# The last eight row tiles of w_down and a second first pair without Strassen, w_down's other blocks two at a time

## The chip, the cores and the metric

The kernel runs on one core of a Trainium2 chip, in one launch. The metric is the device time of one execution in microseconds (us); lower is better. The kernel before took 2080.86 us (median of three runs, 2079.91 to 2081.47).

## What is computed

One layer of a decoder for N = 1056 tokens (1024 of one prompt and 32 of eight samples), D = 1024 features: a SwiGLU half, a token mixer, a second SwiGLU half and a final RMSNorm. In the reference, cut to what the change touches:

```
mod = (silu(c) @ w_ada + b_ada).reshape(B, 9, 1024)
hn = modulate(rmsnorm(x, g_ffn1), mod[0], mod[1])
x  = x + 0.5 * mod[2] * ((silu(hn @ w1_gate) * (hn @ w1_up)) @ w1_down)    # w_gate, w_up 1024x3072, w_down 3072x1024
hn = modulate(rmsnorm(x, g_mix), mod[3], mod[4])
x  = x + mod[5] * (mixer(hn) @ w_mix_out)
hn = modulate(rmsnorm(x, g_ffn2), mod[6], mod[7])
x  = x + 0.5 * mod[8] * ((silu(hn @ w2_gate) * (hn @ w2_up)) @ w2_down)
y  = rmsnorm(x, final_gain)
```

modulate is h * (1 + scale) + shift; every sequence has a conditioning vector c of its own.

## The kernel before

Everything lies feature-major: features on 128 partitions, tokens along the free axis. A float32 operand is split into a high part (an ACT copy to fp32r) and a low part (a DVE subtraction), and a product is three matmuls: high x low, low x high, high x high. The class Stream loads weights through SP's queue into raw buffers and splits them into hl tiles a few units ahead of their use (L175 on ACT, L176 on DVE).

**FFN1 and FFN2.** The feature tiles of 128 go in twelve pairs. In FFN1 the first pair is multiplied directly (first_pair); all later pairs, and all twelve of FFN2, go by Strassen-Winograd (strassen, matmul L365): the operands are cut in 2 x 2 quarters, the token halves being 528 wide, and seven products take the place of eight. A product is 24 matmuls of 264 columns where four tiles of 128 are summed (nk = 4). The hn tiles (hn11, hn21, hn22 and the sums hnT1 to hnT4; hm in FFN2) are the token forms; in FFN2 token_forms (L560 to L579) makes the sums on ACT and DVE from x after the norm. gate_up takes all seven products of the gate (ga) and then all seven of up, and combine (L374 to L384) takes them out of three double PSUM tiles a, c, b: ACT copies the first three (L378), DVE adds later ones to the copies (L383). The results, or their seven token forms, are stored to HBM (store, L650 to L674, on POOL's queue).

**w_down** reads these forms back in groups of feature tiles (GROUPS, L78): pairs 0 to 3, 4 to 7 and 8 to 9, by Strassen with nk = 4, 4 and 2. Within a group the block o = 0 to 3 gives two of the eight output tiles. load_form (L713 to L721) reads a form of the next group, 1056 KB, as soon as the last block's product has freed its buffer, and splits it (ACT L720, DVE L721). down takes the seven products out by combine into temporaries, and adds these to x (L584 and, for the first token half, L758; L588 and L590 for the samples). x itself was dropped during gate and up and is loaded again (L792) into the place of gate_up's temporaries. The last pairs, 10 and 11 (LAST_PAIR), are four row tiles of w_down multiplied directly, by back_by_span over spans of tokens (bk, matmul L327 of 352 columns), so that the next norm can begin on the first span while PE works on the others. last_m (L762 to L771) loads and splits what they multiply (ml).

**Beside it** runs the modulation: ada steps (L408) of eight matmuls each, one every third product, from weights of their own (raw<-wada).

**From the mixer to FFN2** back_by_span goes by quarters of 264 tokens (QUARTERS); x is normed in place into hm and kept (L530 to L535), then token_forms makes the sums, and FFN2's pair 0 begins (ga0).

The order on each engine is the order of the program as a tile scheduler leaves it; every engine runs its own list in order. The diff touches:

Of the kernel before, what the change touches and what calls it, by code (L numbers as in the profile page):

```python
# [14 lines left out]
P = 128  # L15
# [6 lines left out]
N = T + S  # L22
# [55 lines left out]
GROUPS = ((0, 4), (4, 4), (8, 2))  # L78
LAST_PAIR = 10
# [3 lines left out]
class Stream:  # L83


    def __init__(self, nc, rawp, hlp, sums, raw_bufs, plan, srcs):
# [3 lines left out]
        for kind, idx in plan:  # L90
            if kind in ("ga1", "ga2", "dn1", "dn2"):
                self.add_strassen(kind, idx, srcs[kind](idx))
                continue
            b = dict(key=(kind, idx), src=srcs[kind](idx), raw=None, ids=[])
            if kind in ("gu1", "mi"):
# [17 lines left out]
        self.dma = self.split = self.done = self.pos = 0  # L113

    def add_strassen(self, kind, idx, srcs):

        at = len(self.blocks)
        nk = srcs[0].shape[-2]
        blocks = list(range(at, at + len(srcs)))
        for i, src in enumerate(srcs):  # L120
            self.blocks.append(dict(key=(kind, idx) if i == 0 else None, src=src, raw=None, ids=[], left=1,
                                    shape=list(src.shape)))
        self.blocks[at]["ids"] = list(range(len(self.units), len(self.units) + 7))
        self.blocks[at]["span"] = len(srcs)
        sums = {}

        def quarter(raws, m, k):
            return raws[k][:, m - 1] if len(raws) == 2 else raws[0][:, k, m - 1]

        def make(form):  # L130
            def f(raws):
                if form in ("11", "12", "22"):
                    return quarter(raws if len(raws) > 1 else raws * len(blocks), int(form[0]), int(form[1]) - 1)
                w11, w12, w21, w22 = (quarter(raws, m, k) for m in (1, 2) for k in (0, 1))
                t = self.sums(f"{form}_{kind}_{at}", nk * P).rearrange("p (k m) -> p k m", k=nk)
# [11 lines left out]
            return f  # L147

        for form in W_FORMS:
            ends = {"S3": blocks[:1] if len(blocks) == 2 else [], "22": blocks[-1:]}.get(form, [])  # L150
            self.units.append(dict(needs=blocks[:1] if form == "11" else blocks, make=make(form), ends=ends, n=nk))

    def dma_ahead(self):
        while self.dma < min(self.done + self.raw_bufs, len(self.blocks)):
            b = self.blocks[self.dma]
            raw = self.rawp.tile(b["shape"], F32, tag="raw", name=f"raw{self.dma}")
            self.nc.sync.dma_start(raw, b["src"])
            b["raw"] = raw
            self.dma += 1
# [7 lines left out]
    def split_to(self, u):  # L167
        while self.split <= min(u, len(self.units) - 1):
# [5 lines left out]
            hl = self.hlp.tile([P, 2, un["n"], P], F32R, tag="hl", name=f"hl{self.split}")  # L174
# [20 lines left out]
def decoder_step(ctx, tc, xin, par, ada0, ada1, ada2, wada, wf, wga1, wga2, wdn1, wdt, wdl, wmi, wgt, wmo,  # L195
# [17 lines left out]
    hlp = open_pool("hlp", bufs=8)  # L213
# [13 lines left out]
    def strassen_banks(on):  # L227

        nonlocal psp
        if not on:  # L230
            close_pool("ps2")
        close_pool("psp")
        if on:
            psp = open_pool("psp", bufs=2, space=bass.MemoryType.PSUM)
            ps2[0] = open_pool("ps2", bufs=3, space=bass.MemoryType.PSUM)
        else:
            psp = open_pool("psp", bufs=8, space=bass.MemoryType.PSUM)
# [33 lines left out]
    def plan_ffn(n):  # L271
        if n == 1:
            plan.extend(("gu1", (i, w)) for i in range(2) for w in range(2))
        plan.extend((f"ga{n}", (p, w)) for p in range(int(n == 1), NP) for w in range(2))
        plan.extend((f"dn{n}", (g, o)) for g in range(len(GROUPS)) for o in range(4))
        plan.extend((f"d{n}", h) for h in range(4))
# [10 lines left out]
    def down_src(n):  # L287
        def f(i):
            g, o = i
            return [wdn1[n, g, o, 0], wdn1[n, g, o, 1]] if GROUPS[g][1] == 4 else [wdt[n, o]]  # L290
        return f

    ws = Stream(nc, rawp, hlp, lambda name, width: tmp(name, width), 2, plan, dict(
        gu1=lambda i: wf[i[0], i[1]], ga1=lambda i: [wga1[i[0] - 1, i[1], h] for h in range(2)],
        ga2=lambda i: [wga2[i[0], i[1], h] for h in range(2)], dn1=down_src(0), dn2=down_src(1),
        d1=lambda h: wdl[0, h], d2=lambda h: wdl[1, h],
# [50 lines left out]
    def halves(b):  # L347
        return b[:, :, 0:Q]

    def two(t):  # L350
        return t.rearrange("p (q c) -> p q c", q=2)

    def strassen(name, ids, forms, nk, after, done=lambda i: None):

        banks = {}
        for i in range(7):
            hl = ws.unit(ids[i], AHEAD_S)
            new = BANK_OF[i] not in banks
            if new:
                banks[BANK_OF[i]] = ps2[0].tile([P, 2, 512], F32, tag="ps2", name=f"{name}_{BANK_OF[i]}")  # L360
            b = banks[BANK_OF[i]]
            for q in range(2):
                for k in range(nk):
                    for j, (wh, h) in enumerate(((0, 0), (0, 1), (1, 0))):
                        pe.matmul(b[:, q, 0:Q], hl[:, wh, k], forms[X_FORMS[i]][:, k, h, q * Q:q * Q + Q],  # L365
                                  start=new and k == 0 and j == 0, stop=k == nk - 1 and j == 2, skip_group_check=True)
            after(i, banks)
            done(i)
            advance()
# [980 lines left out]
```

## Time and profile before

| | |
|---|---|
| median of three runs | 2080.86 us |
| the profiled execution: its own time | 2083.96 us |
| its span | 2082.0 us |
| PE, DVE, ACT, POOL busy | 95%, 65%, 39%, 6% of the span |
| time by kind of DMA | f<-mf 1056 KB: 7.5 us to landing; raw<-wga 512 KB: 3.4 us |

A row of the timeline is one run of like instructions on an engine: start, duration, line, tiles, count, and in brackets the idle time just before it and what ended it. The rows of PE tell where its work stood still; the windows tell which engine was busy there.

### The profile page before, as it was taken

The page shows a single profiled execution, that of the slowest core. Times are in us where ns is not written, and L with a number is a line of the kernel's source. Part 1 is how long each engine was busy: PE and PEld are TensorE (multiplying, and loading weights), DVE is VectorE, ACT ScalarE, POOL GpSimd, SP SyncE. Part 2 cuts the span into 40 slices and gives each one's busy share as a digit, 9 for nine tenths or more (in the row PEclk, how much of TensorE's full clock was granted, in tenths as well). Part 3 has the DMA queues.
Part 4 walks back from the last instruction along what each step waited for, and adds up shares of the span by engine and source line. Part 5 has one row for each costly group of instructions (what it writes and reads, how often), then busy time and mean ns, then how long its engine had stood idle before and what let it go on. Part 6 is the DMA issues. An engine that isn't in the chain of part 4 may idle for free.

```text
span 2082.0 us, 36792 instructions
## 1 busy us (share of the span) xinstructions
PE 1975.9 (95%) x15256; PEld 1922.7 (92%) x15256; DVE 1361.1 (65%) x2633; ACT 806.6 (39%) x1435; POOL 132.8 (6%) x233
## 2 busy tenths in 40 slices
PE   5999999999989898999999986999999999999897
PEld 4989999999979898999999984999999999999897
DVE  6864554655466758776767788556555655777686
ACT  5433332333343425444434334333333333443453
POOL 0010000010020000000000000001000100110100
PEclk9999999999989999999999996999999999999998
DMA  7144333444381413110111111422222322751312
GB/s 281 37 174 144 138 129 128 145 149 147 122 309 61 179 59 147 63 56 26 51 51 42 53 63 72 148 88 106 106 88 88 124 88 93 271 184 62 148 52 84
DMA packets 70998, 237.18 MB, mean 114 GB/s; under 512 B 7952, under 2 KB 14096, under 8 KB 70832
## 3 DMA queue, kind: packets, MB, share of 16 engines
q1 hardware_dynamic: 44128, 137.40, 19.3%
q0 software_dynamic: 26704, 97.45, 12.6%
q8 instruction: 119, 1.95, 0.4%
q14 instruction: 47, 0.39, 0.1%
HBM read 183.88 MB, written 50.93 MB: 113 GB/s over the span
## 4 chain that ended last, share of the span: by engine, by line
PE 80%; DVE 9%; issue 6%; DMA 4%; ACT 1%; POOL 0%; DVEq 0%; SPq 0%; ACTq 0%; POOLq 0%
PE ga_a L365 13%; PE up_a L365 12%; PE bk L327 9%; PE dn_a L365 7%; PE ga_c L365 6%; PE up_c L365 6%; PE dn_c L365 3%; PE ga_b L365 3%; PE up_b L365 3%; PE v L327 2%; PE b L327 2%; PE c L327 2%; PE x L327 2%; DMA f<-mf 2%; PE ada L408 2%
## 5 line engine op out<-in xcount | busy, mean ns | idle before, releaser
L175 ACT ACTIVATE hl<-raw 128x512 fp32r<-128x512 f32 (+1 forms) x292 | 174.0, 610 | 308.6 <-PE up_a L365 68.6
L365 PE MATMUL dn_a<-f,hl 128*128 128x264 f32 x1920 | 254.5, 289 | 22.9 <-ACT f L720 10.6
L176 DVE TENSOR_TENSOR hl<-raw,hl 128x512 fp32r<-128x512 f32 (+1 forms) x292 | 191.3, 667 | 127.1 <-ACT hl L175 125.8
L365 PEld LDWEIGHTS dn_a<-f,hl 128*128 128x128 f32 x1920 | 243.6, 191 | 27.8 <-ACT f L720 11.0
L176 DVE TENSOR_TENSOR hl<-S_ga,hl 128x512 fp32r<-128x512 f32 x184 | 126.1, 690 | 114.8 <-ACT hl L175 113.7
L175 ACT ACTIVATE hl<-S_ga 128x512 fp32r<-128x512 f32 x184 | 115.5, 629 | 158.2 <-issue 57.2
L365 PE MATMUL dn_c<-f,hl 128*128 128x264 f32 x960 | 133.7, 296 | 7.8 <-DVE d_3st L383 7.5
L365 PEld LDWEIGHTS dn_c<-f,hl 128*128 128x128 f32 x960 | 127.3, 198 | 10.8 <-issue 5.4
L175 ACT ACTIVATE hl<-S_dn 128x512 fp32r<-128x512 f32 (+1 forms) x96 | 53.0, 559 | 175.5 <-DVE x L590 73.3
L365 PE MATMUL ga_a<-hmT,hl 128*128 128x264 f32 x864 | 113.0, 287 | 2.8 <-ACT g0st L378 2.8
L365 PEld LDWEIGHTS ga_a<-hmT,hl 128*128 128x128 f32 x864 | 109.1, 190 | 3.9 <-ACT g0st L378 3.1
L365 PE MATMUL up_a<-hmT,hl 128*128 128x264 f32 x864 | 111.6, 285 | 0.7 <-DVE u11st L383 0.7
L365 PEld LDWEIGHTS up_a<-hmT,hl 128*128 128x128 f32 x864 | 107.7, 188 | 1.9 <-DVE u11st L383 0.9
L365 PEld LDWEIGHTS up_a<-hnT,hl 128*128 128x128 f32 x792 | 100.0, 191 | 6.8 <-issue 4.5
L365 PE MATMUL up_a<-hnT,hl 128*128 128x264 f32 x792 | 104.6, 289 | 1.8 <-DVE u11st L383 1.8
L365 PE MATMUL ga_a<-hnT,hl 128*128 128x264 f32 x792 | 103.0, 286 | 0.0
L365 PEld LDWEIGHTS ga_a<-hnT,hl 128*128 128x128 f32 x792 | 98.5, 188 | 4.5 <-issue 4.5
L721 DVE TENSOR_TENSOR f<-f 128x1056 fp32r<-128x1056 f32 x70 | 85.6, 1255 | 22.0 <-ACT f L720 21.8
L327 PE MATMUL bk<-ml,hl 128*128 128x352 f32 (+2 forms) x672 | 97.5, 305 | 0.0
L327 PEld LDWEIGHTS bk<-ml,hl 128*128 128x128 f32 x672 | 95.1, 192 | 0.0
L720 ACT ACTIVATE f<-f 128x1056 fp32r<-128x1056 f32 x70 | 72.8, 1078 | 42.5 <-DMA f<-mf 42.4
L584 DVE SCALAR_TENSOR_TENSOR x<-bk,modT,x 128x352 f32<-128x352 f32 (+6 forms) x112 | 56.5, 520 | 40.0 <-PE bk L327 39.3
(492 smaller groups left out, 3841.6 us busy)
## 6 DMA issues: line engine op xcount, KB each, us to landing
raw<-wga SPq DMA_DIRECT2D x92, 512.0 KB, 3.4
f<-mf POOLq DMA_DIRECT2D x28, 1056.0 KB, 7.5
raw<-wada SPq DMA_DIRECT2D x56, 512.0 KB, 3.4
raw<-wdn SPq DMA_DIRECT2D x32, 512.0 KB, 3.4
mf<-mt POOLq DMA_DIRECT2D x60, 264.0 KB, 3.5
raw<-wmi SPq DMA_DIRECT2D x20, 512.0 KB, 3.3
f<-mf POOLq DMA_DIRECT2D x14, 528.0 KB, 8.3
raw<-ada SPq DMA_DIRECT2D x16, 384.0 KB, 7.9
```

Source lines behind the costliest of these rows:

```text
L175: self.nc.scalar.activation(hl[:, 0], src, AF.Copy)
L176: self.nc.vector.tensor_sub(hl[:, 1], src, hl[:, 0].bitcast(F32))
L327: pe.matmul(b[:, :sp[1]], hl[:, wh, k], rhs(k, h, sp), start=first and k == ks[0] and i == 0, stop=last and k == ks[-1] and i == 2)
L365: pe.matmul(b[:, q, 0:Q], hl[:, wh, k], forms[X_FORMS[i]][:, k, h, q * Q:q * Q + Q], start=new and k == 0 and j == 0, stop=k == nk - 1 and ...
L408: pe.matmul(ada_bank[u][32 * q:32 * q + 32, :ADA_W[u]], cst[:, k], raw[:, q], start=k == 0, stop=k == KD - 1, skip_group_check=True)
L584: dve.scalar_tensor_tensor(x[:, o, lo:lo + n], b[:, :n], modT[:, buf, GATE, o, 0:1], x[:, o, lo:lo + n], op0=ALU.mult, op1=ALU.add)
L720: act.activation(form[:, k:k + 2, 0], raw[:, k:k + 2], AF.Copy)
L721: dve.tensor_sub(form[:, k:k + 2, 1], raw[:, k:k + 2], form[:, k:k + 2, 0].bitcast(F32))
```

## The change

Four things, in both FFNs where nothing else is said:

1. w_down's last eight row tiles instead of four are multiplied directly: the group of pairs 8 and 9 (nk = 2) is gone, and its four row tiles go by back in spans of 352 columns ahead of back_by_span on the other four.
2. FFN2's first pair is multiplied directly, too (second_pair), quarter by quarter as the norm of each quarter is flushed; the token forms T1, T2 and T4 are made as side work of it, T3 behind it (third_form).
3. strassen takes two jobs side by side: product i of the one, then product i of the other, out of four double PSUM tiles. So go w_down's blocks o and o + 1, and the last pair's gate and up. A double PSUM tile is now read as 528 columns in one piece, and a product of w_down is added to x straight from it, wherever it belongs, so that the copies, temporaries and adds of combine fall away there.
4. The kept copy of the normed x (L535) goes from DVE to ACT; five raw buffers in place of two during an FFN's Strassen part; six hl buffers (eight outside); three ada steps a call in place of two, so that none is left after pair 8.

```diff
-GROUPS = ((0, 4), (4, 4), (8, 2))
-LAST_PAIR = 10
+GROUPS = ((0, 4), (4, 4))
+LAST_PAIR = 8
...
-    hlp = open_pool("hlp", bufs=8)
+    hlp = open_pool("hlp", bufs=6)
...
-            ps2[0] = open_pool("ps2", bufs=3, space=bass.MemoryType.PSUM)
+            ps2[0] = open_pool("ps2", bufs=doubles, space=bass.MemoryType.PSUM)
...
+            ws.rotate("raw", [rawp] * 2 + [open_pool("raw2", bufs=3)] * 3)
+            ws.raw_bufs = 5
...
-    def strassen(name, ids, forms, nk, after, done=lambda i: None):
+    def strassen(jobs, forms, nk, done=lambda i: None):
...
-        banks = {}
+        banks = [{} for _ in jobs]
         for i in range(7):
-            hl = ws.unit(ids[i], AHEAD_S)
...
+            for (name, ids, after), bs in zip(jobs, banks):
+                hl = ws.unit(ids[i], AHEAD_S + len(jobs) - 1)
...
+                after(i, bs)
+                advance()
+                if len(adas[1]) > adas[2] and i % 2 == 1:
+                    more_ada()
             done(i)
-            advance()
-            if len(adas[1]) > adas[2] and i % 3 == 1:
-                more_ada()
...
         if keep:
-            dve.tensor_scalar_add(h, h, shift)
+            act.activation(h, h, AF.Identity, bias=shift)
...
-            for o in range(4):
-                temps = {}
...
-                def add(i, banks):
-                    r = combine(temps, fresh, i, banks)
-                    if r:
-                        f, h, t = r
-                        add_half(buf, 2 * o + f, h, two(t) if i < 6 else t, t if i < 6 else None)
+            for o in (0, 2):
+                ids = ws.take(f"dn{n}", ((g, o), (g, o + 1)))
...
+                def add(o):
+                    def after(i, banks):
+                        f, hs = ((0, (0,)), (1, (1,)), (0, (1,)), (0, (1,)), (1, (1,)), (0, (0,)), (1, (0,)))[i]
+                        for h in hs:
+                            add_back(buf, 2 * o + f, (h * HALF, HALF), whole(banks[BANK_OF[i]]))
+                    return after
...
+                strassen([(f"dn{g}_{o + j}", ids[j], add(o + j)) for j in range(2)], forms, nk, done)
             forms = nxt
...
-        down(n, buf, nxt, ms, form_pools)
-        close_pool("f2")
-        strassen_banks(False)
-        last(f"d{n}", buf, ms[0])
+        down(n, buf, nxt)
...
+        ms = [last_m(m0, n, 0), last_m(mps[0], n, 1)]
+        strassen_banks(0)
+        back(f"d{n}", 0, buf, ms[0])
+        close_pool("m0")
+        last(f"d{n}", buf, ms[1])
...
+    def second_pair():
+        ms = [[(wide if i == 0 else lambda name: tmp(name, HALF))(f"n{i}_{h}") for h in range(2)] for i in range(2)]
+        ids = [[ws.take("gu2", (i, w)) for w in range(2)] for i in range(2)]
+        for c, sp in enumerate(QUARTERS):
+            flush(("n", sp))
+            if c % 2:
+                side.append((("tf", c), token_forms(forms, c // 2, Q)))
+            for i in range(2):
...
+                for w in range(2):
+                    j = 2 * (2 * i + w)
+                    gb, = from_hn(ids[i][w], f"n{i}{w}", [sp], (min(AHEAD, 6 - j), 0, 0, 6)[c])
+                    if w == 0:
+                        act.activation(m, gb[:, :Q], AF.Silu)
+                    else:
+                        dve.tensor_mul(m, m, gb[:, :Q])
+        flush()
+        return [*ms[0], *ms[1]]
```

Three places show how the instructions move. First TensorE in w_down's group 0 (before: the end of block 0 and the start of block 1; `dn0_1_c` is bank c of block 1, `f1_0_2` the third form of group 0 in FFN1):

```order
L365 MATMUL dn0_0_a_6434<-f1_0_4_6296,hl166_6463 128x264 x24
L365 MATMUL dn0_0_b_6595<-f1_0_5_6340,hl167_6495 128x264 x24
L365 MATMUL dn0_0_a_6434<-f1_0_6_6376,hl168_6524 128x264 x24
L365 MATMUL dn0_1_a_6657<-f1_0_0_6143,hl169_6558 128x264 x24
L365 MATMUL dn0_1_c_6691<-f1_0_1_6183,hl170_6592 128x264 x24
L365 MATMUL dn0_1_a_6657<-f1_0_2_6224,hl171_6624 128x264 x24
L365 MATMUL dn0_1_c_6691<-f1_0_3_6261,hl172_6654 128x264 x24
```

and of the changed kernel, blocks 2 and 3 of the same group:

```order
L396 MATMUL dn0_2_a_6879<-f1_0_0_5997,hl176_6756 128x264 x24
L396 MATMUL dn0_3_a_6910<-f1_0_0_5997,hl177_6785 128x264 x24
L396 MATMUL dn0_2_c_6947<-f1_0_1_6067,hl178_6816 128x264 x24
L396 MATMUL dn0_3_c_6981<-f1_0_1_6067,hl179_6846 128x264 x24
L396 MATMUL dn0_2_a_6879<-f1_0_2_6139,hl180_6876 128x264 x24
L396 MATMUL dn0_3_a_6910<-f1_0_2_6139,hl181_6907 128x264 x24
L396 MATMUL dn0_2_c_6947<-f1_0_3_6203,hl182_6944 128x264 x24
L396 MATMUL dn0_3_c_6981<-f1_0_3_6203,hl183_6978 128x264 x24
```

Each form is now used by two products in a row, and two products of other banks lie between two on the same bank.

Next VectorE where group 0's last blocks run and group 1's forms are split (`f1_1_0 x2` is one form's two subtractions; `d0_3st2` a temporary of combine). Before:

```order
L721 TENSOR_TENSOR f1_1_0_7130<-f1_1_0_7130 128x2x528 x2
L383 TENSOR_TENSOR d0_3st2_7203<-dn0_3_c_7143,d0_3st2_7203 128x528
L721 TENSOR_TENSOR f1_1_1_7170<-f1_1_1_7170 128x2x528 x2
L584 SCALAR_TENSOR_TENSOR x1_6417<-d0_3st2_7203,modT_81,x1_6417 128x496
L588 TENSOR_TENSOR ab6_7242<-d0_3st2_7203,modT_81 128x32
L383 TENSOR_TENSOR d0_3st1_7168<-dn0_3_a_7103,d0_3st1_7168 128x528
L721 TENSOR_TENSOR f1_1_2_7205<-f1_1_2_7205 128x2x528 x2
L590 TENSOR_TENSOR x1_6417<-x1_6417,ab6_7242 128x32
L584 SCALAR_TENSOR_TENSOR x1_6417<-d0_3st1_7168,modT_81,x1_6417 128x496
```

and the changed kernel:

```order
L758 TENSOR_TENSOR f1_1_1_7010<-f1_1_1_7010 128x2x528 x2
L193 TENSOR_TENSOR hl185_7053<-S3_dn1_52_1_7051,hl185_7053 128x512
L626 TENSOR_TENSOR ab6_7083<-dn0_3_a_6910,modT_81 128x32
L193 TENSOR_TENSOR hl186_7092<-raw54_6598,hl186_7092 128x512
L628 TENSOR_TENSOR x1_6419<-x1_6419,ab6_7083 128x32
L622 SCALAR_TENSOR_TENSOR x1_6419<-dn0_2_c_6947,modT_81,x1_6419 128x496
L626 TENSOR_TENSOR ab4_7120<-dn0_2_c_6947,modT_81 128x32
L193 TENSOR_TENSOR hl187_7123<-raw55_6693,hl187_7123 128x512
L628 TENSOR_TENSOR x1_6419<-x1_6419,ab4_7120 128x32
L622 SCALAR_TENSOR_TENSOR x1_6419<-dn0_3_c_6981,modT_81,x1_6419 128x496
L758 TENSOR_TENSOR f1_1_2_7086<-f1_1_2_7086 128x2x528 x2
```

Before, one or two places lie from one form's split to the next, with combine's add and the add to x as an instruction each; now nine lie between two forms, the splits of weights among them, and the source of each add to x is PSUM.

Last TensorE between the mixer's last product and FFN2 (`nrm792` and `rb792` belong to the norm of the last quarter; `hl312` and the like are split weights). Before:

```order
L472 MATMUL nrm792_13060<-ones_79,sq792_7_13050 128x1
L493 MATMUL rb792_13093<-dg792_13077,ones_79 128x128 x2
L493 MATMUL rb792_13093<-dg792_13077,ones_79 128x8
L365 MATMUL ga0_a_13286<-hm11_12326,hl312_12968 128x264 x24
L365 MATMUL ga0_c_13320<-hmT1_13139,hl313_13002 128x264 x24
L365 MATMUL ga0_a_13286<-hmT2_13140,hl314_13031 128x264 x20
L408 MATMUL ada9_13347<-raw0_13270,cst_83 32x256 x4
L365 MATMUL ga0_a_13286<-hmT2_13140,hl314_13031 128x264 x4
```

and the changed kernel, where `n01_0` is the first tile's up product on the quarter that begins at token 0:

```order
L504 MATMUL nrm792_12947<-ones_79,sq792_7_12885 128x1
L357 MATMUL n01_0_12973<-hm21_12153,hl295_12906 128x264 x9
L357 MATMUL n10_0_13015<-hm11_12151,hl296_12911 128x264 x12
L357 MATMUL n10_0_13015<-hm21_12153,hl297_12930 128x264 x12
L525 MATMUL rb792_13028<-dg792_12964,ones_79 128x128 x2
L525 MATMUL rb792_13028<-dg792_12964,ones_79 128x8
L357 MATMUL n11_0_13054<-hm11_12151,hl298_12974 128x264 x12
L357 MATMUL n11_0_13054<-hm21_12153,hl299_12993 128x264 x12
L357 MATMUL n00_528_13091<-hm12_12157,hl292_12805 128x264 x12
```

Products on the earlier quarters now lie ahead of, between and behind the steps of the last quarter's norm; before, the first product that needs no sum of quarters stands behind all of them, and the second needs hmT1.

## Rows read from the trace of the kernel before

**Rows 1.** The page, its part 1: busy time, share of the span, instructions.

```profile
PE 1975.9 (95%) x15256; PEld 1922.7 (92%) x15256; DVE 1361.1 (65%) x2633; ACT 806.6 (39%) x1435; POOL 132.8 (6%) x233
```

**Rows 2.** Windows; columns: window, length, PE, PEld, DVE, ACT, POOL busy (instructions), clock, DMA.

```profile
680.00:714.00 34.00, 26.41 (x189) 25.38 (x189) 29.32 (x38) 19.73 (x25) 3.00 (x4) 0.90 0.61 225
...
780.00:815.00 35.00, 27.62 (x198) 25.91 (x197) 31.44 (x57) 19.67 (x32) 4.99 (x8) 0.90 0.52 196
...
1240.00:1260.00 20.00, 11.08 (x65) 10.54 (x63) 18.22 (x59) 7.14 (x16) 0.84 (x1) 0.74 0.16 56
...
1260.00:1280.00 20.00, 8.02 (x18) 4.74 (x18) 19.97 (x60) 10.59 (x26) 0.00 (x0) 0.61 0.00 0
...
1955.00:1985.00 30.00, 22.67 (x150) 21.14 (x149) 26.14 (x42) 18.16 (x28) 4.87 (x7) 0.83 0.54 210
```

**Rows 3.** Timeline of PE, first Strassen product of FFN1.

```profile
108.82 5.50 PE L365 MATMUL ga_c<-hnT,hl 128*128 128x264 f32 x24 [7.56 <-DVE m L861]
```

**Rows 4.** Timeline of PE, FFN1's last up, and the first blocks of w_down.

```profile
570.20 3.09 PE L365 MATMUL up_a<-hn,hl 128*128 128x264 f32 x24
...
573.13 3.09 PE L365 MATMUL up_c<-hnT,hl 128*128 128x264 f32 x24
...
576.14 0.64 PE L408 MATMUL ada<-raw,cst 128*32 128x256 f32 x8
...
606.44 1.08 PE L408 MATMUL ada<-raw,cst 128*32 128x256 f32 x8 [3.78 <-DMA raw<-wada]
```

**Rows 5.** Timeline of PE, change from group 0 to 1, and the direct tiles.

```profile
699.46 5.43 PE L365 MATMUL dn_c<-f,hl 128*128 128x264 f32 x24 [3.77 <-DVE d_3st L383]
...
835.67 4.54 PE L327 MATMUL bk<-ml,hl 128*128 128x352 f32 x27
...
835.83 19.41 PE L327 MATMUL bk<-ml,hl 128*128 128x352 f32 x119
```

**Rows 6.** Timeline of PE, FFN2's last up, group 1 to 2, and the direct tiles.

```profile
1761.43 3.09 PE L365 MATMUL up_a<-hm,hl 128*128 128x264 f32 x24
...
1963.85 0.59 PE L365 MATMUL dn_a<-f,hl 128*128 128x264 f32 x1 [5.51 <-ACT f L720]
...
2011.33 3.84 PE L327 MATMUL bk<-ml,hl 128*128 128x272 f32 x29
```

**Rows 7.** Timeline of PE, from the mixer's last product to FFN2's pair 1.

```profile
1241.45 0.53 PE L327 MATMUL bk<-mix_s,hl 128*128 128x264 f32 x3
...
1255.45 4.10 PE L365 MATMUL ga_a<-hm,hl 128*128 128x264 f32 x24
...
1288.62 4.05 PE L365 MATMUL ga_a<-hmT,hl 128*128 128x264 f32 x20 [2.81 <-ACT g0st L378]
...
1328.20 3.09 PE L365 MATMUL ga_a<-hm,hl 128*128 128x264 f32 x24
```

**Rows 8.** Groups of DVE's instructions by form: busy, mean ns, idle.

```profile
L721 DVE TENSOR_TENSOR f<-f 128x1056 fp32r<-128x1056 f32 x70 | 85.6, 1255 | 22.0 <-ACT f L720 21.8
...
L758 DVE SCALAR_TENSOR_TENSOR x<-dn_a,modT,x 128x528 f32<-128x528 f32 x24 | 18.3, 764 | 0.0
...
L584 DVE SCALAR_TENSOR_TENSOR x<-d_0st,modT,x 128x496 f32<-128x496 f32 x12 | 8.8, 732 | 2.1 <-issue 1.9
...
L579 DVE TENSOR_TENSOR hmT<-t2f,hmT 128x264 fp32r<-128x264 f32 x16 | 7.1, 442 | 0.0
...
L535 DVE TENSOR_SCALAR x<-x,modT 128x264 f32<-128x264 f32 x24 | 8.4, 352 | 0.0
```

**Rows 9.** Timeline of POOL and DVE, FFN2's load of x.

```profile
1787.77 0.71 DVE L703 TENSOR_TENSOR g11s<-g11s,up_a 128x528 f32<-128x528 f32 x1
...
1793.84 4.34 POOL L792 DMA_DIRECT2D x<-xmid  x8 [3.51 <-DMA ml<-g11st]
...
1799.45 0.73 DVE L584 SCALAR_TENSOR_TENSOR x<-d_0st,modT,x 128x496 f32<-128x496 f32 x1 [1.86 <-issue]
```

**Rows 10.** View of the tile ml, in FFN1's w_down.

```profile
DMA to landing us min/median/max: 6.5/6.5/6.5
```

More of the change, by code (lines that the diff above doesn't have):

```diff
@@ L113, in __init__, with rotate, maker, make @@
         self.dma = self.split = self.done = self.pos = 0
+        self.slots = dict(raw=[[rawp], 0], hl=[[hlp], 0])
+    def rotate(self, tag, more=None):
+        s = self.slots[tag]
+        if more is not None:
+            s[:] = [more, 0]
+            return
+        s[1] += 1
+        return s[0][(s[1] - 1) % len(s[0])]
     def add_strassen(self, kind, idx, srcs):
         at = len(self.blocks)
[L118 to L131, printed above, removed]
+        nj = len(srcs)
+        nk = srcs[0][0].shape[-2]
+        for k in range(2):
+            for src in srcs:
+                self.blocks.append(dict(key=None, src=src[k], raw=None, left=1, pair=True, shape=list(src[k].shape)))
+        first = self.blocks[at]
+        first.update(key=(kind, idx), span=2 * nj, ids=[[len(self.units) + nj * i + j for i in range(7)] for j in range(nj)])
+        def maker(j):
+            sums = {}
+            def make(form, raws):
                 if form in ("11", "12", "22"):
-                    return quarter(raws if len(raws) > 1 else raws * len(blocks), int(form[0]), int(form[1]) - 1)
-                w11, w12, w21, w22 = (quarter(raws, m, k) for m in (1, 2) for k in (0, 1))
-                t = self.sums(f"{form}_{kind}_{at}", nk * P).rearrange("p (k m) -> p k m", k=nk)
+                    return raws[-1 if form[1] == "2" else 0][:, int(form[0]) - 1]
+                w11, w12, w21, w22 = (raws[k][:, m] for m in range(2) for k in range(2))
+                t = self.sums(f"{form}_{kind}_{at}_{j}", nk * P).rearrange("p (k m) -> p k m", k=nk)
                 sub, add = self.nc.vector.tensor_sub, self.nc.vector.tensor_add
@@ L155, in dma_ahead @@
             b = self.blocks[self.dma]
-            raw = self.rawp.tile(b["shape"], F32, tag="raw", name=f"raw{self.dma}")
+            if len(self.slots["raw"][0]) > 1 and not b.get("pair"):
+                self.rotate("raw", [self.rawp])
+                self.raw_bufs = 2
+                continue
+            raw = self.rotate("raw").tile(b["shape"], F32, tag="raw", name=f"raw{self.dma}")
             self.nc.sync.dma_start(raw, b["src"])
@@ L173, in split_to @@
             src = un["make"](raws)
-            hl = self.hlp.tile([P, 2, un["n"], P], F32R, tag="hl", name=f"hl{self.split}")
+            hl = self.rotate("hl").tile([P, 2, un["n"], P], F32R, tag="hl", name=f"hl{self.split}")
             self.nc.scalar.activation(hl[:, 0], src, AF.Copy)
@@ L344, in hn_rhs, with whole @@
         return lambda k, h, sp: hn_at(4 * half + k, h, *sp)
[L347 to L351, printed above, removed]
-    def strassen(name, ids, forms, nk, after, done=lambda i: None):
-        banks = {}
-        for i in range(7):
-            hl = ws.unit(ids[i], AHEAD_S)
[L358 to L367, printed above, removed]
+    def whole(b):
+        return b[:, 512 - Q:512 + Q]
@@ L680, in wide, with gate_up @@
         return widep[0].tile([P, HALF], F32, tag="u", name=name)
-    def gate_up(n, p, forms, done=lambda i: None):
-        ids = [ws.take(f"ga{n}", (p, w)) for w in range(2)]
+    def gate_up(n, p, forms, done):
         sg, ms = {}, {}
```

267 lines of the change are left out of this document (143 added, 124 removed).

## The prediction

> **What bounds the kernel now.** I read the busy shares first: PE is busy 95% of the span, DVE 65%, ACT 39% [rows 1]. So the time is PE's work plus the stretches in which PE stands still or runs slowly, and the question of each edit is what it does to either. PE's timeline, read through once, has its gaps at few places: behind FFN1's directly multiplied pair, from gate and up to w_down, at each change of group in w_down, and from the mixer to FFN2. The windows over these [rows 2] show who is late there: at the first change of group DVE is busy 29.3 us of 34 and PE 26.4, at the second DVE 31.4 of 35, and behind the mixer DVE 18.2 and then 20.0 us of 20 while PE has 11.1 and 8.0 at granted clocks of 0.74 and 0.61. The last idle times there name DVE's combine, ACT's and DVE's form splits, and a late ada weight [rows 4 to 6]. These are the places the change rebuilds. In between PE runs through: 24 matmuls of 264 columns take 573.13 - 570.20 = 2.93 us [rows 4], 0.122 us each, and 119 of 352 columns take 19.41 us less a tail of some 0.2, 0.162 us each [rows 5].
>
> **The matmuls.** Per FFN the group of nk = 2 had 4 blocks x 7 products x 12 = 336 matmuls of 264 columns, 41.0 us; four row tiles multiplied directly are 4 x 8 x 3 x 3 = 288 of 352 columns, 46.6 us. So w_down costs 5.6 us more in each FFN. FFN2's first pair goes from 14 x 24 = 336 to 384 matmuls (2 tiles x 2 weights x 8 x 3 x 4 quarters) of 264 columns, 5.9 us more. Together 17.1 us of PE work is added. All that can be won is in the gaps.
>
> **FFN1, from the last pair's up to the direct tiles.** In the trace this is 835.67 - 570.20 = 265.5 us [rows 4, 5]. Six ada steps of about 0.6 us stand in it [rows 4] (the step at 576.14 to the one at 606.44 are the first and the last); they move to earlier pairs and cost the same there, so 262.1 us is to be compared. Without any gap it would be 7 x 2.93 = 20.5 for up and 1680 x 0.122 = 205.3 for w_down, 225.8; so 36 us are lost. In the changed kernel the work is 20.5 + 8 blocks x 7 x 2.93 = 164.1 and 46.6 for the four more direct tiles: 231.2 us. Which gaps stay:
> - A form of the next group was loaded every 2.9 us, while DVE needs 2 x 1.255 = 2.5 us for its split [rows 8] and has products to take out and weights to split beside it: that is why DVE is late at both changes. Two blocks side by side use a form for 5.9 us, so the last loads are asked for twice as far apart and the first of them 41 us, not 20, ahead of the next group. DVE has 7 x 2.5 = 17.5 us of forms and some 26 us of the rest in 41 us (14 products with an add of 0.76, a split of about 0.7 and a share of a weight sum). That is more than full, but the last forms are needed only late in the next pair of blocks, so I cost the change at nothing; without that cover it costs up to 5 us, like the wait in [rows 6]. The second change is gone with its group.
> - The wait for ada weights (3.78 us, [rows 4]) goes, as no ada step is left there.
> - x is loaded again behind the last store of the last pair: in FFN2 of the trace the last product of up was multiplied into g11s at 1787.77, the load issued at 1793.84 after 3.51 us of waiting for a store, and the first add to x began at 1799.45, 11.7 us after the mul [rows 9]. In the changed kernel the first product's add stands first in DVE's list, and behind it the next splits of weights. PE can run four products, 11.7 us, until it must write the first bank again. The mul comes 0.7 to 3.4 us behind the last product, so PE waits between 0 and 6 us (below, if the load starts no later than its forerunner's store; above, if x comes behind a form and raw tiles on the same DMA engines). I take 2.5.
> - The four new m tiles are loaded (landing 6.5 us, [rows 10]) and split on ACT and DVE (1.25 us, the width of a form half). In FFN1 the buffers come free 5.9 us before w_down ends, so PE waits 1 to 4 us; I take 2. Half a microsecond for the rest.
>
> So 236.2 us against 262.1: 25.9 won, between 13 (half of today's losses stay) and 31 (none).
>
> **FFN2, the same stretch.** 2011.33 - 1761.43 = 249.9 us [rows 6] without ada steps, so 24 are lost, 5.51 of them behind ACT's split. The work becomes 231.2 as well. x costs 2.5 again; here three of the m tiles wait for w_down's very last product, so landing and split lie open but for the first tile's 1.5 us of work: 4 to 9 us, I take 6. 239.7 against 249.9: 10.2 won, between 3 and 19.
>
> **The adds from PSUM.** DVE had 4 adds to x and 3 adds of combine a block, 4 of the 7 with a source in PSUM; now it has 7 adds to x, all from PSUM, and ACT's 3 copies are gone. An add of 528 from PSUM takes 764 ns, one of 496 from the copy in SBUF 732 [rows 8]: 32 columns for 32 ns, so the source costs nothing that the row shows.
> [...]
>
> **From the mixer to FFN2.** The mixer's last product ends at about 1242.0, and pair 1 starts at 1328.20: 86.2 us [rows 7] for 41 us of products and four ada steps (2.4), with two sums of quarters in between that PE waits for one by one. In the changed kernel 384 matmuls, 46.8 us, stand there, and three quarters' norms are done when the mixer ends. They need no sums of quarters. DVE has about as much to do as before: the kept copies go to ACT (29 x 0.35 us less, [rows 8]), T3 goes in four pieces of 528 instead of eight of 264 and later, and there are splits for the hm low parts, 11 more weight units of about 0.7 and 8 muls: about +3 us net. So the first quarter, whose last four weight units queue behind DVE, is through some 6 us late, at 1242.0 + 11.7 + 6 = 1259.7; the other three take 35.1 us, and pair 1 can begin at 1294.8. T3 is needed only 11.7 us later. Won: 1328.2 - 2.4 - 1294.8 = 31.0 us. Bounds: 37 if PE runs through (1288.8), and 23 if the first quarter is multiplied at the lower clock throughout and DVE is late once more: 24 matmuls took 5.43 us next to a wait [rows 5] instead of 2.93, so 96 cost up to 10 us more.
> The windows show the clock at 0.61 to 0.74 where PE has 8 to 11 us of work in 20 [rows 2]. [...]
>
> **FFN1's first pair.** PE waits 7.56 us for the last mul before the first sum of quarters, and this product runs 5.50 us [rows 3]. One weight unit less is split ahead of it: 0.5 us won, between -2 and 4. The kept copy on ACT costs nothing there: ACT is idle 61% of the span. Six hl buffers hold the four units that are split ahead; if they don't suffice, PE waits for weights at many units, and the first rival has that price.
>
> **Sum.** 31.0 + 25.9 + 10.2 + 0.5 = 67.6 us, in which the 17.1 us of more work is already paid. The profiled execution took 2083.96 us (span 2082.0 and 2.0 around it), 3.1 above the median of the runs. So 2083.96 - 67.6 - 3.1 = 2013.
>
> **Rivals.**
> - *Half the gaps come back in a new place* (DVE's list blocked on x and on forms that land late beside five raw buffers and 4.3 MB of x; the quarters held up by the norm). For it: DVE is 86 to 100% busy at these places [rows 2]; against it: forms have twice the distance. Low ends: 23 + 13 + 3 - 1 = 38 won, 2043; middle of these and mine, 53 won, about 2028.
> - *No gaps at all*: 37 + 31 + 19 + 4 = 91 won, 1990. For it: four PSUM pairs and 41 us of lead. Against it: x and m are loads that nothing covers in full.
> - *Slower*: DVE, not the order, sets the length of these stretches. If its work at each change takes as long as the stretch does today, then nothing of the gaps goes and the matmuls come on top: 2080.9 + 17.1 = 2098. This decides where an add from PSUM holds its bank so long that DVE needs over 3.5 us a product: 7 splits, sums and adds of 0.6 to 0.8 make about 2.1 now, so the add would have to take three times its 764 ns [rows 8]. Idle time of DVE in the windows (4.7 us of 34, 3.6 of 35) speaks against it.
> - *The change does not do what it says*: the quarters don't run beside the norm, as DVE has 20 of 20 us [rows 2]; then the first part wins nothing and loses 5.9, about 2050.
>
> **How the numbers follow.** Forecast 55%; half the gaps 22%; none 13%; no overlap 4%; slower 5%, and 1% that gains and losses meet within 0.2% (4 us, about what a measurement of this kernel can tell from no change). So faster 0.94, same 0.01, slower 0.05. The forecast's own range is 2003 to 2024; with the two neighbours in part 1994 to 2040.
>
> **What would show it.** Right: from the end of the mixer to pair 1 about 53 us with PE over 85% busy; no idle over 1 us at the change of group; from the start of FFN1's pair 11 to the direct tiles about 257 us; single waits of 2 to 6 us behind the load of x and at FFN2's first direct tile. Wrong: PE waiting for DVE within w_down's second pair of blocks, or a clock under 0.8 throughout the first 40 us behind the mixer.

## The result and the profile after

The changed kernel takes 2026.64 us (median of four runs, 2024.15 to 2028.84) beside 2080.39 for the kernel before on the same chip; the ratio is 0.9743 [0.9726, 0.9760]. In a second set of four runs it took 2023.83 us, ratio 0.9732 [0.9706, 0.9757]. Over all eight runs the median is 2025.4, and that is what "the changed kernel" means below. It is faster by 55 us where 68 were forecast, and its time lies just above the forecast's own range, 2003 to 2024. The profiled execution took 2028.84 us, with a span of 2027.1. The page's busy shares, beside [rows 1]:

```profile
PE 1966.1 (97%) x15208; PEld 1923.5 (95%) x15208; DVE 1285.9 (63%) x2528; ACT 768.7 (38%) x1368; POOL 120.7 (6%) x215
```

PE has 48 matmul records fewer and is busy 10 us less, although 17 us of matmuls came on top: a matmul that runs at a lower granted clock counts as longer work (the 24 of [rows 5] took 5.43 us, with the clock at 0.54 from 699 to 705 us; [rows 4] have 3.09 at 1.00), and there is less of that now: the mean granted clock is 0.988, where it was 0.972. By stretches of the two profiled executions, cut at the same instructions:

| stretch | before, us | after, us | won |
|---|---|---|---|
| start to the first Strassen product | 98.1 | 95.1 | 3.0 |
| FFN1: the last up to the first statistic of the next norm | 284.9 | 260.9 | 24.0, 20.5 without six moved ada steps |
| from there to the mixer's last product (unchanged code) | 386.7 | 389.8 | -2.9 |
| the mixer's last product to FFN2's pair 1 | 86.4 | 53.7 | 32.7 |
| pairs 1 to 11 of FFN2 | 454.9 | 459.8 | -4.9, -2.6 without four moved ada steps |
| FFN2's w_down to the first statistic of the last norm | 243.4 | 237.3 | 6.1 |

Not in the table are FFN1's Strassen pairs up to the last up (-3.9, of which 3.5 are the six ada steps that moved there) and the end behind the last statistic (+1.2); with them the stretches give the 54.9 us by which the span fell, but for 0.4 at the cuts.

PE's timeline in FFN1, where [rows 4, 5] had the gaps (start, duration, line, tiles, count, idle before):

```profile
591.64 6.02 PE L396 MATMUL dn_a<-f,hl 128*128 128x264 f32 x48
597.49 6.01 PE L396 MATMUL dn_c<-f,hl 128*128 128x264 f32 x48
608.08 7.63 PE L396 MATMUL dn_a<-f,hl 128*128 128x264 f32 x48 [4.57 <-DVE x L622]
...
674.21 11.90 PE L396 MATMUL dn_a<-f,hl 128*128 128x264 f32 x96
...
764.06 0.91 PE L357 MATMUL bk<-ml,hl 128*128 128x352 f32 x4 [1.69 <-ACT ml L789]
```

Between the first blocks and the direct tiles PE does not wait once; the change of group lies inside the row at 674.21. What is left are the two waits that the prediction had put there, for x at 608.08 and for the m tiles at 764.06. FFN2 has the same two, beside [rows 6], and behind the second of them two more for m tiles, of 0.38 and 0.86 us:

```profile
1750.27 7.62 PE L396 MATMUL dn_a<-f,hl 128*128 128x264 f32 x48 [3.02 <-DVE x L622]
...
1906.55 0.91 PE L357 MATMUL bk<-ml,hl 128*128 128x352 f32 x4 [1.69 <-ACT ml L789]
```

The windows that answer to [rows 2], for the change of group and the 40 us behind the mixer (window, length, PE, PEld, DVE, ACT, POOL busy, clock, DMA):

```profile
660.00:694.00 34.00, 34.00 (x280) 34.00 (x279) 31.62 (x50) 15.97 (x21) 3.00 (x4) 1.00 0.57 203
...
1222.00:1242.00 20.00, 18.16 (x135) 17.59 (x134) 16.07 (x49) 16.07 (x33) 0.85 (x1) 0.91 0.50 160
1242.00:1262.00 20.00, 20.00 (x166) 20.00 (x165) 18.65 (x52) 13.43 (x35) 0.56 (x1) 1.00 0.05 16
```

At the change of group DVE is busier than before (31.6 us of 34, [rows 2] 29.3) and PE no longer waits for it. Behind the mixer PE is busy 18 and 20 us of 20, where it had 11 and 8. PE's rows there, beside [rows 7]:

```profile
1224.98 0.58 PE L504 MATMUL nrm<-ones,sq 128*128 128x1 f32 x4
...
1227.32 1.62 PE L504 MATMUL nrm<-ones,sq 128*128 128x1 f32 x14
...
1230.60 2.93 PE L357 MATMUL n<-hm,hl 128*128 128x264 f32 x22 [0.21 <-DVE hl L193]
1235.12 0.81 PE L525 MATMUL rb<-dg,ones 128*128 128x128 f32 x6 [1.59 <-DVE dg L518]
1235.78 39.96 PE L357 MATMUL n<-hm,hl 128*128 128x264 f32 x312
1275.58 3.07 PE L396 MATMUL ga_a<-hm,hl 128*128 128x264 f32 x24
...
1298.38 3.18 PE L396 MATMUL ga_a<-hmT,hl 128*128 128x264 f32 x24 [2.16 <-DVE g1st L415]
```

From 1235.78 on 312 matmuls run in one piece. The wait at 1298.38, in pair 1, is new.

The other signs came too, but for one: from the start of FFN1's pair 11 to the last four direct tiles it is 262 us, where about 257 stood.

### The profile page after: what moved, and what is told of

Its sections match the earlier page's. It is cut to its first block, busy times and chain, and to the rows that moved or that the text cites. A ratio compares the mean times of both kernels' runs of the same rounds, so it can differ in the third digit from the quotient of the medians.

```text
span 2027.1 us, 36531 instructions
## 1 busy us (share of the span) xinstructions
PE 1966.1 (97%) x15208; PEld 1923.5 (95%) x15208; DVE 1285.9 (63%) x2528; ACT 768.7 (38%) x1368; POOL 120.7 (6%) x215
## 4 chain that ended last, share of the span: by engine, by line
PE 89%; DVE 5%; issue 2%; DMA 2%; ACT 1%; POOL 0%; DVEq 0%; SPq 0%; POOLq 0%; ACTq 0%
PE bk L357 14%; PE up_a L396 13%; PE ga_a L396 12%; PE dn_a L396 9%; PE up_c L396 6%; PE ga_c L396 6%; PE dn_c L396 4%; PE up_b L396 3%; PE ga_b L396 3%; PE v L357 2%; PE dn_b L396 2%; PE b L357 2%; PE c L357 2%; PE x L357 2%; PE g L357 2%
## 5 line engine op out<-in xcount | busy, mean ns | idle before, releaser
L193 DVE TENSOR_TENSOR hl<-raw,hl 128x512 fp32r<-128x512 f32 x286 | 195.5, 687 | 214.0 <-ACT hl L192 213.5
L192 ACT ACTIVATE hl<-raw 128x512 fp32r<-128x512 f32 x286 | 176.9, 626 | 276.5 <-PE bk L357 100.9
L396 PE MATMUL dn_a<-f,hl 128*128 128x264 f32 x1536 | 195.4, 287 | 7.7 <-DVE x L622 7.6
L396 PEld LDWEIGHTS dn_a<-f,hl 128*128 128x128 f32 x1536 | 192.5, 191 | 8.2 <-issue 8.2
L357 PE MATMUL bk<-ml,hl 128*128 128x352 f32 (+2 forms) x1248 | 194.3, 316 | 5.1 <-ACT ml L789 4.2
L357 PEld LDWEIGHTS bk<-ml,hl 128*128 128x128 f32 x1248 | 190.1, 192 | 7.0 <-ACT ml L789 5.1
L193 DVE TENSOR_TENSOR hl<-S_ga,hl 128x512 fp32r<-128x512 f32 x176 | 121.0, 690 | 87.1 <-ACT hl L192 86.4
L622 DVE SCALAR_TENSOR_TENSOR x<-bk,modT,x 128x352 f32<-128x352 f32 (+6 forms) x160 | 81.4, 534 | 96.6 <-PE bk L357 95.5
L396 PE MATMUL dn_c<-f,hl 128*128 128x264 f32 x768 | 96.5, 284 | 0.0
L396 PEld LDWEIGHTS dn_c<-f,hl 128*128 128x128 f32 x768 | 94.9, 188 | 0.0
L192 ACT ACTIVATE hl<-S_dn 128x512 fp32r<-128x512 f32 x64 | 39.8, 628 | 128.6 <-DVE S_dn L151 36.8
L758 DVE TENSOR_TENSOR f<-f 128x1056 fp32r<-128x1056 f32 x56 | 67.9, 1253 | 28.8 <-ACT f L757 28.6
```

What stands on the lines that cost most here:

```text
L192: self.nc.scalar.activation(hl[:, 0], src, AF.Copy)
L193: self.nc.vector.tensor_sub(hl[:, 1], src, hl[:, 0].bitcast(F32))
L357: pe.matmul(b[:, :sp[1]], hl[:, wh, k], rhs(k, h, sp), start=first and k == ks[0] and i == 0, stop=last and k == ks[-1] and i == 2)
L396: pe.matmul(b[:, 512 - Q + q * Q:512 + q * Q], hl[:, wh, k], forms[X_FORMS[i]][:, k, h, q * Q:q * Q + Q], start=new and k == 0 and j == 0, ...
L622: dve.scalar_tensor_tensor(x[:, o, lo:lo + n], b[:, :n], modT[:, buf, GATE, o, 0:1], x[:, o, lo:lo + n], op0=ALU.mult, op1=ALU.add)
L758: dve.tensor_sub(form[:, k:k + 2, 1], raw[:, k:k + 2], form[:, k:k + 2, 0].bitcast(F32))
```

## The experiments

Each starts from the changed kernel (2025.4 us) and changes one thing in it, but for the run of the two loads behind x, which builds on the run before it, and the three at the end, which join edits. A time is the median of its runs, a ratio is to the kernel before on the same chip. The runs were made on four chips, on which the kernel before took 2078.6 to 2081.9 us, and single runs of the changed kernel lie between 2018 and 2029 us; so a difference of a few us between two medians shows little by itself.

**The changed kernel again.** 

> The changed kernel as it is, once more. Theory (chance in the clock): 2024 to 2029 us again, but the stretches at a lower granted clock that had no wait before them (870 to 890 us and 1190 to 1210 us of the first profile, some 4 us lost in the mixer) lie elsewhere or are missing; the mixer's part from the first norm after w_down to its last product takes 386 to 390 us. Rival (the change itself slows the mixer): the clock falls at the same two places again and the part takes 390 us.

2023.83 us (2018.06 to 2027.14); the profiled execution has a span of 2016.3, 10.8 less than the first. The mixer's part took 385.0 us where the first profile had 389.8. The same window, in which the two are at the same place of the program to a tenth of a microsecond, after and then in this run:

```profile
866.00:886.00 20.00, 18.41 (x93) 18.15 (x92) 14.09 (x38) 6.48 (x14) 0.00 (x0) 0.74 0.10 36
```

```profile
866.00:886.00 20.00, 18.41 (x122) 18.15 (x121) 17.49 (x47) 9.15 (x20) 0.00 (x0) 1.00 0.11 37
```

PE is busy 18.41 us in both and gets 93 matmuls done in the one and 122 in the other. So the loss at 870 us is the clock's and not the change's. At the second place, 1193 to 1213 us, the clock was 0.91 in both profiles, but it fell behind the norm of one quarter in the first (at 1199 us) and of the next quarter in the second (at 1208 us); the kernel before has 0.91 in its like window, 1205 to 1225. The rival is out for the stretch as a whole.

**FFN2's first pair by Strassen.** Edit: the plan of gu2, second_pair and its weights taken out, the token forms made after the norm.

```
-        plan.extend((f"gu{n}", (i, w)) for i in range(2) for w in range(2))
+        if n == 1:
+            plan.extend(("gu1", (i, w)) for i in range(2) for w in range(2))
...
-    ms = second_pair()
+    for q in range(2):
+        for _ in token_forms(forms, q, Q):
+            pass
```

> FFN2's first pair by Strassen again, everything else as changed. Theory (PE has products that need no sums while DVE makes the norm and the sums): the stretch from the mixer's last product to pair 1 goes from 54 us to 80 to 86, and the time rises by 26 to 32 us, to about 2055. Rival (what shortened it is DVE's smaller load: the kept copy on ACT, T3 in wide pieces and last): it rises by 10 us at most, to 2036.

2044.87 us, ratio 0.9839 [0.9817, 0.9861], 19 us more. The stretch to pair 1 took 82.0 us. PE's rows:

```profile
1235.17 5.25 PE L397 MATMUL ga_a<-hm,hl 128*128 128x264 f32 x24 [0.18 <-DVE x L563]
...
1249.68 1.38 PE L397 MATMUL ga_c<-hmT,hl 128*128 128x264 f32 x3 [0.68 <-ACT hmT L617]
...
1262.71 2.35 PE L397 MATMUL ga_a<-hmT,hl 128*128 128x264 f32 x9 [5.45 <-ACT g0st L411]
```

The gaps of the kernel before are back, three matmuls at a time. But pairs 1 to 11 took 452.2 us here and 459.8 in the changed kernel, so 7.6 of the 28 us are given back there, 3.4 of them only because six ada steps lie in the first pair here. The theory holds, its price was too high. The rival's part is small: with DVE's smaller load the stretch took 82.0 us here and 86.4 in the kernel before.

**One at a time.** Edit: `for o in range(4)` in down with one job a call, gate and then up in the last pair, each block planned alone; adds from PSUM stay. With one job a call the weights are also split three units ahead, as in the kernel before, and not four.

> w_down's blocks one at a time, and the last pair's gate and up one after the other; products are still added to x from PSUM. Theory (a form must last two products for DVE to keep up): PE waits 8 to 15 us at the start of w_down and as much at its change of group in each FFN, and the time rises by 20 to 40 us, to about 2055. Rival (the adds straight from PSUM, without copies and temporaries, removed the waits): it stays within 5 us, to 2031 at most.

2079.81 us, ratio 1.0004 [0.9992, 1.0017]: the whole gain is gone. From w_down's first product to the next norm's statistic it took 268.6 us in FFN1 and 265.7 in FFN2, 28 us more each, of which 2.9 are up's last product, which lies within it here. The two largest waits of FFN1:

```profile
607.40 3.01 PE L395 MATMUL dn_b<-f,hl 128*128 128x264 f32 x12 [3.57 <-DVE hl L193]
```

```profile
704.70 5.62 PE L395 MATMUL dn_a<-f,hl 128*128 128x264 f32 x24 [6.64 <-ACT hl L192]
```

They lie where [rows 4, 5] had theirs, and the waits are for the splits of weights behind the splits of forms. The rival is out: the adds from PSUM remove no wait by themselves. The theory was right in kind; the loss was larger than its upper end of 40. It is also larger than what w_down had won: in FFN2 of the kernel before, cut in the same way, the stretch took 247.3 us, 18 less than here. 5.6 us of that are the direct tiles' matmuls. For the rest, PE stood still for 15.2 us within the products of groups 0 and 1 here, and for 7.4 in the kernel before. So the other edits make w_down slower when its blocks go one at a time, and the pairing carries them; which of them does it, and what the one unit of lead is worth alone, was not tried.

**Only the last pair one after the other.** Edit: the part of the last one in gate_up and the plan.

> Only the last pair's gate and up one after the other again, w_down's blocks side by side as changed. Theory (the first group's forms are then asked for 20 us ahead and every 2.9 us, and DVE and POOL are late for the first blocks): 6 to 25 us more than the changed kernel, 2031 to 2050, with waits in group 0's first products. Rival (all of the loss of the run with both one at a time is in w_down's own order): within 4 us.

2032.33 us (2025.24 to 2037.79), ratio 0.9765 [0.9743, 0.9787], about 7 more, not far outside the scatter. PE's waits of the whole run that the changed kernel does not have, and the wait for x, which is 7.6 us there:

```profile
PE dn_c L395 <- DVE hl L193: 5.0, 2, 2.8
PE up_a L395 <- DVE u11st L414: 4.8, 2, 2.9
...
PE dn_a L395 <- DVE x L621: 2.7, 2, 1.6
```

The waits of the theory are there; of their 9.8 us 4.9 come back at x, where PE waits 2.7. Of the loss of 54 us with both, some 7 are the last pair's and the rest, some 47, w_down's.

**The third group by Strassen again**, two blocks side by side. Edit, beside an order of the hl buffers that fits it:

```
-GROUPS = ((0, 4), (4, 4))
-LAST_PAIR = 8
+GROUPS = ((0, 4), (4, 4), (8, 2))
+LAST_PAIR = 10
```

> Pairs 8 and 9 of w_down by Strassen again (two tiles summed, two blocks side by side), four direct row tiles as before the change. It has 11.2 us of matmuls less. Theory (a product of 1.46 us gives DVE less time than its add, split and sums need, about 1.6 us): the group takes 45 us or more per FFN against 46.6 for the direct tiles, and the time is 2018 to 2030. Rival (two blocks side by side hide DVE there too, so that the direct tiles are 11 us given away): 2013 to 2017.

2014.49 us, ratio 0.9693 [0.9667, 0.9719], 11 us less than the changed kernel. The end of the group in FFN1:

```profile
795.93 3.10 PE L399 MATMUL dn_a<-f,hl 128*128 128x264 f32 x24
798.86 3.10 PE L399 MATMUL dn_b<-f,hl 128*128 128x264 f32 x24
801.79 3.09 PE L399 MATMUL dn_a<-f,hl 128*128 128x264 f32 x24
807.65 0.88 PE L360 MATMUL bk<-ml,hl 128*128 128x352 f32 x4 [2.77 <-ACT ml L792]
```

Here 24 matmuls are two products of 12, one of each block, and run at 2.93 us. So the rival is right: DVE keeps up at the short products, and both changes of group go without a wait. The direct tiles' 11.2 us of matmuls are given away. In the profile the two stretches of w_down got 7.6 us shorter; of the rest a part went into longer waits: PE waited 9.3 us for x here and 7.6 in the changed kernel, and 2.77 us for FFN1's first m tile where it had waited 1.69.

**The kept copy on DVE.** Edit: `act.activation(h, h, AF.Identity, bias=shift)` back to `dve.tensor_scalar_add(h, h, shift)`.

> The kept copy of the normed x on DVE again. Theory (behind the mixer the weights' splits queue behind DVE, so 29 instructions of 0.35 us more make the first quarter's products late): the stretch from the mixer's last product to pair 1 grows by 3 to 8 us, the time by 2 to 8 us against the changed kernel. Rival (the products of the other quarters cover it): nothing within 2 us.

2031.06 us, ratio 0.9763 [0.9745, 0.9781], some 5 more, with an interval that overlaps that of the changed kernel. But the stretch to pair 1 took 55.4 us, 1.7 more only; the first Strassen product of FFN1 began at 98.99 us, as in the kernel before, and not at 95.13. PE's waits for the first norm, in this run and in the changed kernel:

```profile
PE first L856 <- ACT hn L564: 2.4, 4, 1.4
```

```profile
PE first L856 <- ACT hn L564: 0.9, 2, 0.6
```

These rows carry 1.5 us of the 3.9, and a spell at a clock of 0.83 at 60 to 70 us, where the changed kernel has 1.00, some of the rest. So the theory has the wrong place: the copy mattered in FFN1's first norm. How much it is worth there is open: in the twelve profiles with the copy on ACT this product began between 94.50 and 97.40 us, in the two with it on DVE at 98.12 and 98.99.

**The last store out of the way of x.** Edit:

```
-                sg[f, h] = wide(f"g{p}s") if i == 6 else t
+                sg[f, h] = t if i < 6 else wide(f"g{p}s") if done is None else tmp(f"g{p}s", HALF)
```

> The last product's gate tile of each FFN's last pair lies in a buffer that x does not need, so that x's load no longer waits for its store. Theory (in the chain last mul, store, load of x, first add, the store is 3 us, but then the split of the last form stands ahead of the first add): the two waits for the first add shrink from 7.3 us together to 2 to 5, the time falls by 2 to 6 us. Rival (the first add waits for DVE's queue, not for the load): no change.

2013.77 us, ratio 0.9682 [0.9667, 0.9697], 12 less. The two waits for the first add:

```profile
PE dn_a L396 <- DVE x L622: 1.7, 2, 1.2
```

They were 7.6 us. The spells at a lower clock at 600 to 620 and 1750 to 1760 us are gone with them: the mean clock was 0.91 and 0.83 there in the changed kernel and is 1.00 here. The theory holds; with the clock its price was too low.

**Two forms loaded behind x**, beside the last edit. Edit: forms 5 and 6 of group 0 are issued after the load of x.

> As the run with the moved last store, and the loads of the last two forms of group 0 are issued behind the load of x instead of ahead of it. Theory (load and split of these forms are what else stands ahead of the first add): both waits go, and with them the half-speed spells behind them: 7.3 us of waiting and some 3 of slow clock, so 8 to 11 us less than the changed kernel, 2013 to 2017. Rival (4.3 MB of x then delay the forms, which are needed 29 us later): the wait comes back at the b bank's product, no gain.

2014.22 us, ratio 0.9683 [0.9666, 0.9699]. Both waits are gone:

```profile
606.13 6.02 PE L396 MATMUL dn_a<-f,hl 128*128 128x264 f32 x48
```

But the time is that of the run before: the 1.7 us that were left don't show in the runs.

**FFN2's first direct tiles in the early buffers.** Edit: `at = (m0, mps[0]) if n == 1 else (mps[0], m0)` for the two sets of m tiles.

> In FFN2 the direct tiles that are multiplied first are loaded into the buffers that come free early, the others into those that come free with the last product. Theory: FFN2's wait at the first direct tile (2.9 us and a spell at half clock behind it) goes, 3 to 6 us less. Rival (the weights of the direct tiles are late too): the wait stays, 0 to 1 us less.

2015.30 us (2012.19 to 2021.74), ratio 0.9692 [0.9670, 0.9714]. PE's wait for these tiles is FFN1's alone,

```profile
PE bk L357 <- ACT ml L789: 1.7, 1, 1.7
```

and the stretch from the end of w_down to the first statistic went from 67.9 us to 62.4, 5.5 less. The other 4 to 5 us of the median have no place in the trace that would be this edit's; the executions differ by as much.

**Together.** Three runs put the gains together. The third group and the store:

> Pairs 8 and 9 by Strassen again, two blocks side by side, and the last store moved out of the way of x's load. Theory (both gains are at places of their own: 9 us of matmuls and 11 us of waits): about 2004, 2000 to 2008. Rival (what the shorter waits gave was the clock's chance): 2011 to 2015.

2005.58 us, ratio 0.9643 [0.9625, 0.9661]. With the two forms behind x as well:

> The same and the last two forms of group 0 loaded behind x. Theory: within 2 us of the run before it in this list, as 1.7 us of waiting were left and two forms are split later. Rival (a wait at every form of group 0): 3 us more or worse.

2002.98 us (2000.38 to 2005.67), ratio 0.9626 [0.9612, 0.9641], the fastest kernel here: 78 us under the one before and 22 under the changed one. It is 2.6 us under the run before, within the scatter of both. The changed kernel with the store and the m tiles:

> The changed kernel with the moved last store and FFN2's first direct tiles in the buffers that come free early. Theory: the two gains add up but for the clock's share, 2003 to 2009. Rival: not below 2012.

2010.10 us, ratio 0.9659 [0.9637, 0.9680], above the theory's range by a microsecond.

## Why the prediction was right, and where its sum was off

**The bound** was right: the gain is PE's gaps, less the matmuls. The places that the prediction names changed the way it says, and 54.9 us of span are won, of 67.6 forecast. Most of the 13 us between them were lost in w_down of the two FFNs and in pair 1, and the time came out nearer to the first rival's than to the forecast's 2013. By its terms:

- *The group changes at nothing.* Right, by the window at 660 to 694 and the row at 674.21. But the prediction also wrote "the second change is gone with its group", as if the direct tiles had taken that gap away. The run with the third group shows that side-by-side blocks do it without the direct tiles: the group and the change to it ran at the matmuls' own pace, and the run was 11 us faster, where the direct tiles cost 11.2 by matmuls.
- *x, 2.5 us per FFN.* This is the term most mis-sized. The chain was the right one, as rows of POOL and DVE of the changed kernel show, beside [rows 9]:

```profile
599.32 0.56 POOL L694 DMA_DIRECT2D ml<-g11s  x1 [3.46 <-DVE g11s L735]
602.90 4.19 POOL L813 DMA_DIRECT2D x<-xin  x8 [3.02 <-DMA ml<-g11s]
```

```profile
598.33 0.69 DVE L735 TENSOR_TENSOR g11s<-g11s,up_a 128x528 f32<-128x528 f32 x1
...
602.57 2.43 DVE L758 TENSOR_TENSOR f<-f 128x1056 fp32r<-128x1056 f32 x2 [2.34 <-ACT f L757]
607.16 0.77 DVE L622 SCALAR_TENSOR_TENSOR x<-dn_a,modT,x 128x528 f32<-128x528 f32 x1 [2.17 <-DMA x<-xin]
```

The last up product made way for w_down at 591.64, and its mul began 6.7 us later, not 0.7 to 3.4: DVE had the splits of a form and of weights ahead of it. From the mul to the first add it was 8.8 us more; the add did not stand first in DVE's list, as the prediction has it, but behind two more splits of weights and the last form's. PE had 11.7 us to go on and stood still 4.57 us in FFN1 and 3.02 in FFN2. The 48 products behind each wait took 7.6 us instead of 6.0, with the granted clock at 0.50 from 609 to 611 us and from 1752 to 1755. The prediction left out the slow products behind the wait, though it had itself read some at [rows 5] (5.43 us for 24, behind 3.77 us of idle time). Together that is 11 us against 5, and taking the store away brought 12.
- *The m tiles, 2 and 6 us.* FFN1 lost 3.8 us behind w_down's end, half of it in slow matmuls (clock 0.66 from 764 to 768 us), and FFN2 6.3 (0.50 from 1911 to 1915): the one close to its upper bound of 4, the other as taken. (The 6.5 us of [rows 10] are the slowest of four loads, which landed after 4.1 to 6.5.)
- *FFN1 and FFN2* come to 20.5 and 6.1 by these two, where 25.9 and 10.2 stood.
- *From the mixer to pair 1, 31.0 net.* The stretch took 53.7 us, as forecast to a microsecond (52.8). That it is so close is in part luck: the 6 us of delay were to be weights that queue behind DVE, and PE waited only 0.21 us for weights. In their place stand a wait of 1.59 us for the norm's tile dg, some 2.6 us of the norm's own one-column and 128-column matmuls, which the sum had left out, and a clock of 0.91 in the first 20 us. What was missed is pair 1: its rows show 2.16 us for a combine and 0.79 for an ada weight. DVE stood for 4.41 us just before, waiting for a raw tile of wga, so the combine was late for lack of weights and not of DVE. 28 us are left, and the run without this part says 19 in the runs.
- *FFN1's first pair, 0.5.* 3.0 us were won ahead of the first Strassen product, about as much as this start moves from profile to profile (94.50 to 97.40). The wait in it stayed, 7.49 us and a product of 5.04 ([rows 3] 7.56 and 5.50):

```profile
105.75 5.04 PE L396 MATMUL ga_c<-hnT,hl 128*128 128x264 f32 x24 [7.49 <-DVE m L876]
```

The copy on ACT, which I had costed at nothing there, seems to be part of it. The kernel before had a spell at 0.79 to 0.87 of the clock at 40 to 60 us as well; what share each has is open.
- *Stretches that the change doesn't touch* were taken as equal. The mixer lost 2.9 us in this execution and nothing in the next. That is not a step of the change; it is the scatter of the clock (0.74 and 1.00 from 866 to 886 us in the two), and one profiled execution can't tell the two apart.
- *The adds from PSUM* cost what the row said. In the changed kernel, by form:

```profile
L622 DVE SCALAR_TENSOR_TENSOR x<-dn_a,modT,x 128x528 f32<-128x528 f32 x32 | 24.5, 766 | 33.6 <-PE dn_a L396 29.1 <-issue 2.2 <-DMA x<-xin 2.2
L622 DVE SCALAR_TENSOR_TENSOR x<-dn_a,modT,x 128x496 f32<-128x496 f32 x32 | 23.4, 730 | 12.3 <-PE dn_a L396 12.3
```

Here 496 columns from PSUM take 730 ns, and [rows 8] has 732 from SBUF.

Of the rivals, *half the gaps come back* came nearest by its number (2028), and by none of its reasons but x: forms were not late, and the quarters ran beside the norm. *Slower* needed adds of three times 764 ns. In the prediction's sums two slips moved nothing: the low ends add -1 for FFN1's first pair, whose bound is -2, and 31 less 10 is 21, while 23 stands as the low bound.

## What to carry to other kernels

Where an engine that prepares operands is late only at the changes of a loop, let each operand serve two products in a row before it is dropped. Without that the whole gain of 55 us was gone, with the preparing engine as busy as ever (DVE 33.4 us of the first 44 of FFN1's w_down in both). That is not its share of the gain: by stretches the two w_downs won some 27 us, and without the pairing the other edits made w_down slower than it had been. Price a change part by part, too: the same edit held 11 us of extra matmuls whose gap another part had already closed. And when a new wait is put on PE, count the slower clock behind it (here 7.6 us in place of 6.0 for 48 matmuls, behind waits of 4.57 and 3.02), and look for the one buffer that makes a load wait for a store.

## What the runs showed of the hardware

The same program differed by 10.8 us of span between two profiled executions, and about 8 of them lie in the time that PE was busy at less than the full clock (mean granted clock 0.988 and 0.992). Each of the two has a fall of the granted clock without any wait before it. In the mixer's last part of the changed kernel, PE goes from products to eighteen one-column matmuls of the norm and back:

```profile
1195.96 2.06 PE L504 MATMUL nrm<-ones,sq 128*128 128x1 f32 x18
1197.88 0.62 PE L357 MATMUL bk<-mix_l,hl 128*128 128x264 f32 x3
...
1199.94 0.86 PE L357 MATMUL bk<-mix_l,hl 128*128 128x264 f32 x3
...
1202.42 0.53 PE L357 MATMUL bk<-mix_l,hl 128*128 128x264 f32 x3
```

Three matmuls take 0.66 us from start to start around 1199.94 and 0.37 from 1202.42 on: the granted clock is 0.50 from 1199 to 1202 us and 1.00 in the 10 us before 1198. No row in between has idle time. The second execution has the same behind the next quarter's row:

```profile
1205.60 2.07 PE L504 MATMUL nrm<-ones,sq 128*128 128x1 f32 x18
...
1208.40 0.86 PE L357 MATMUL bk<-mix_l,hl 128*128 128x264 f32 x3
```

The fourteen profiles of this case hold fifteen falls with no idle time of PE just ahead of them, and every one begins within 1.3 us of the end of such a row of eighteen one-column matmuls. 83 other rows of that kind, that at 832.04 us among them, brought no fall. So these falls go with the rows; that the rows are the cause was not tried.
